# Input projection of a hybrid mLSTM / GLA / S5 layer: seven block products for two token blocks, intermediates in DRAM, recurrences in a second phase

## The chip, the cores and the metric

The kernel runs on one core of a Trainium2 chip. The metric is the device time of one execution in microseconds (us). TensorE (PE) multiplies; VectorE (DVE), ScalarE (ACT) and GpSimd (POOL) work elementwise; SyncE (SP) issues nearly all of the kernel's DMAs, in its program order. Each engine runs its own instructions in order and waits on semaphores.

## The reference

One layer on 2048 tokens of width 1024, all in fp32. Normalised tokens are projected to 10264 columns; three recurrences use parts of them; their gated outputs go through three branch matrices and an output matrix.

```python
proj = rmsnorm(x, norm_w) @ w_in                      # [2048,1024] @ [1024,10264]
(aq, ak, av, ao, ai, af, az, bq, bk, bv, ba, bz, cu, cz, g) = split(proj)
qk = silu(causal_dwconv([aq, ak], mlstm_conv))        # 4 taps, 1536 columns
ha = head_norm(mlstm_chunkwise(aq, ak, av, i_pre, logf))   # 4 heads of 192
ya = sigmoid(ao) * ha * silu(az)
yb = head_norm(gla_chunkwise(bq, bk, bv, log_a)) * silu(bz)  # 4 heads, 96 x 192
yc = gelu(s5_ssm(cu, ...)); yc = yc * sigmoid(yc @ s5_w_glu) * silu(cz)
merged = ga * (ya @ w_a) + gb * (yb @ w_b) + gc * (yc @ w_c)   # ga, gb, gc = sigmoid(g)
out = rmsnorm(x + merged @ w_out, final_norm)
```

## The kernel before

Tokens come in four blocks of 512. To keep fp32 accuracy in the fast matmul format, every operand is split into a high part (a rounding copy, on ScalarE) and a low part (the difference, on VectorE or GpSimd, `split`, line 84), and a product of two tiles takes three matmuls: high x high, high x low, low x high. `dense_fm` (line 110, matmuls in lines 122 to 124) gives a result with channels on partitions and 512 tokens in a row; `dense_tm` (line 128, lines 138 to 140) gives one with tokens on partitions, for the values and gates of the recurrences. Both go through the 1024 rows of `w_in` in eight k-tiles; `wload` (line 90) loads each k-tile of weights on SP and splits it, anew for each block.

First comes a stretch that makes the S5 preparation: the four blocks are normalised (`norm`, line 170), the S5 columns u and cz are projected (`proj_c`, with weights kept, names `keep`), the normalised and split blocks go to DRAM (`hnd`), and between them `s5_setup` and `s5_mats` (line 864; tiles P and W, on GpSimd in lines 888 to 891) build the S5 matrices. Then the blocks follow one another: for each, two `gla_pair`s and two `mlstm_pair`s (two heads each, chunks of 64 or 128 tokens), whose queries, keys, values and gates are projected right there, so that matmuls of a projection lie between the steps of a chunk; then three branches with their gates g, and the output projection (`tail`). A chunk of `mlstm_pair` (lines 586 to 646) makes scores (`sp`, line 590), weights them, multiplies by the values (`ni`, line 599) and the state (line 603), transposes the keys, and updates the state `cst` on VectorE (line 625). `s5_main` is mixed into the first block's branches.

The order on each engine is made by the Tile framework when the program is built: it takes the instructions in an order of its own from the code's and the buffers', and a tile's buffers (`bufs`) set how early a producer may run. Names in the rows are tiles: `d` is a PSUM result of a projection, `raw` loaded weights, `whi` and `wlo` their parts, `hn` normalised tokens, `yl` a branch's operand.

## Time and profile before

| | |
|---|---|
| Runs | 3009.79 and 3007.92 us, median 3008.86 |
| Profiled execution: span | 3011.8 us, 41837 instructions |
| TensorE busy | 2868.0 us (95%) |
| VectorE, ScalarE, GpSimd busy | 59%, 42%, 35% |
| DMA | 379.77 MB, mean 126 GB/s |

The page cuts the span into 40 slices of 75.3 us and gives each engine's busy share of a slice in tenths:

```profile
PE   7888899999889899999999999999999999999998
PEld 7667789887667789988888798988888798898886
DVE  7887767645465575665434467565434558556335
ACT  4323544433224554444333544444334554444334
POOL 6788543312240344331122145321122245221022
```

How to read it: where TensorE shows a 9, it is hardly ever waiting, whatever the others do; the slices with 7 and 8 lie at the start. Matmuls are pipelined, so the durations of neighbours overlap: the cost of one in a row of matmuls is the distance from one start to the next, not its duration. A mean over a group that mixes shapes says little, so groups are read by shape.

### The profile page before, as it was taken

The numbers are of one execution on the slowest core, as the hardware profiler recorded it, in microseconds if no ns is written. First come the engines' busy times: TensorE is split into PE (matmuls) and PEld (weight loads), VectorE is DVE, ScalarE is ACT, GpSimd is POOL, SyncE is SP. The second block draws the span as 40 slices with busy tenths as digits, with TensorE's granted clock in tenths as the row PEclk, the third lists the DMA queues.
The fourth block names the chain that finished last, engine by engine and source line by source line (L and its number), as shares of the span: only waits on it lengthen the run. The fifth ranks groups of instructions, "written<-read, shape, count | busy, mean of one in ns | idle before, by whom it ended". The sixth has DMA issues, their size and how long they took to land. (4 is left out here: it accounts for less than half of the span.)

```text
span 3011.8 us, 41837 instructions
## 1 busy us (share of the span) xinstructions
PE 2868.0 (95%) x14360; PEld 2452.7 (81%) x14360; DVE 1785.6 (59%) x3552; ACT 1257.2 (42%) x2512; POOL 1039.8 (35%) x1231
## 2 busy tenths in 40 slices
PE   7888899999889899999999999999999999999998
PEld 7667789887667789988888798988888798898886
DVE  7887767645465575665434467565434558556335
ACT  4323544433224554444333544444334554444334
POOL 6788543312240344331122145321122245221022
PEclk9999999999999999999999999999999999999999
DMA  8734323344777332334445332334445332334433
GB/s 262 254 116 153 108 65 90 91 115 132 210 217 231 121 114 74 86 89 117 135 119 161 120 91 74 94 89 118 138 119 174 98 104 66 99 88 141 148 116 103
DMA packets 279286, 379.77 MB, mean 126 GB/s; under 512 B 82656, under 2 KB 186000, under 8 KB 275744
## 3 DMA queue, kind: packets, MB, share of 16 engines
q1 hardware_dynamic: 273952, 368.70, 41.2%
q10 hardware_dynamic: 5120, 8.39, 1.1%
q8 instruction: 113, 1.85, 0.2%
q14 instruction: 101, 0.83, 0.1%
HBM read 302.33 MB, written 65.04 MB: 122 GB/s over the span
## 5 line engine op out<-in xcount | busy, mean ns | idle before, releaser
L86 DVE TENSOR_TENSOR wlo<-raw,whi 128x512 fp32r<-128x512 f32 (+2 forms) x736 | 548.2, 749 | 764.5 <-ACT whi L85 638.2
L85 ACT CAST whi<-raw 128x512 fp32r<-128x512 f32 (+2 forms) x736 | 421.2, 576 | 716.3 <-PE d L123 412.3
L122 PE MATMUL d<-hn,whi 128*128 128x512 f32 x1472 | 588.4, 400 | 10.1 <-ACT whi L85 8.1
L123 PE MATMUL d<-hn,whi 128*128 128x512 f32 x1472 | 581.7, 395 | 0.0
L124 PE MATMUL d<-hn,wlo 128*128 128x512 f32 x1472 | 553.1, 398 | 9.2 <-DVE wlo L86 8.8
L139 PE MATMUL d<-wlo,hn 128*128 128x384 f32 (+1 forms) x1280 | 442.2, 345 | 11.6 <-POOL wlo L105 6.3
L140 PE MATMUL d<-whi,hn 128*128 128x384 f32 (+1 forms) x1280 | 434.8, 340 | 0.0
L105 POOL TENSOR_TENSOR wlo<-raw,whi 128x384 fp32r<-128x384 f32 x208 | 234.0, 1125 | 518.0 <-ACT whi L104 358.3
L138 PE MATMUL d<-whi,hn 128*128 128x384 f32 (+1 forms) x1280 | 386.6, 348 | 6.9 <-DVE g L299 5.6
L122 PEld LDWEIGHTS d<-hn,whi 128*128 128x128 f32 x1472 | 278.9, 189 | 74.3 <-ACT whi L85 10.4
L124 PEld LDWEIGHTS d<-hn,wlo 128*128 128x128 f32 x1472 | 277.5, 189 | 73.1 <-DVE wlo L86 12.8
L123 PEld LDWEIGHTS d<-hn,whi 128*128 128x128 f32 x1472 | 278.6, 189 | 57.7 <-issue 1.3
L139 PEld LDWEIGHTS d<-wlo,hn 128*128 128x128 f32 x1280 | 243.1, 190 | 18.6 <-DVE wlo L86 7.8
L138 PEld LDWEIGHTS d<-whi,hn 128*128 128x128 f32 x1280 | 236.7, 190 | 15.8 <-DVE g L299 5.9
L140 PEld LDWEIGHTS d<-whi,hn 128*128 128x128 f32 x1280 | 243.2, 190 | 0.4
L669 POOL TENSOR_TENSOR yl<-yraw,yl 128x512 fp32r<-128x512 f32 x64 | 84.7, 1324 | 446.5 <-ACT yl L668 354.5
L122 PE MATMUL d<-yl,whi 128*128 128x512 f32 x512 | 205.6, 403 | 5.1 <-DVE sg L674 1.9
L123 PE MATMUL d<-yl,whi 128*128 128x512 f32 x512 | 202.8, 396 | 0.0
L124 PE MATMUL d<-yl,wlo 128*128 128x512 f32 x512 | 189.6, 399 | 4.7 <-DVE wlo L86 4.7
L104 ACT CAST whi<-raw 128x384 fp32r<-128x384 f32 x208 | 106.1, 510 | 198.4 <-PE d L140 138.5
L679 POOL TENSOR_TENSOR sg<-sg 128x512 f32<-128x512 f32 x64 | 92.8, 1479 | 107.3 <-DVE sg L674 107.3
L539 DVE SCALAR_TENSOR_TENSOR cacc<-craw,convw,cacc 128x512 f32<-128x512 f32 x144 | 120.9, 840 | 2.7
(311 smaller groups left out, 4846.7 us busy)
## 6 DMA issues: line engine op xcount, KB each, us to landing
raw<-in_w_in_dram SPq DMA_DIRECT2D x480, 192.0 KB
raw<-in_w_in_dram SPq DMA_DIRECT2D x232, 256.0 KB
yraw<-y_a SPq DMA_DIRECT2D x64, 256.0 KB
raw<-in_w_out_dram SPq DMA_DIRECT2D x64, 256.0 KB
hnd<-hn SPq DMA_DIRECT2D x6, 2048.0 KB
y_a<-ys SPq DMA_DIRECT2D x64, 192.0 KB
raw<-in_w_bb_dram SPq DMA_DIRECT2D x48, 256.0 KB
raw<-in_w_ba_dram SPq DMA_DIRECT2D x48, 256.0 KB
```

Source lines behind the costliest of these rows:

```text
L85: nc.scalar.copy(out=hi, in_=src)
L86: nc.vector.tensor_tensor(out=lo, in0=src, in1=hi.bitcast(F32), op=ALU.subtract)
L104: nc.scalar.copy(out=hi[:, 0:n], in_=raw[:, 0:n])
L105: nc.gpsimd.tensor_tensor(out=lo[:, 0:n], in0=raw[:, 0:n], in1=hi[:, 0:n].bitcast(F32), op=ALU.subtract)
L122: nc.tensor.matmul(pm, lhsT=hi[:, o:o + mm], rhs=rh[:, ts], start=(k == 0), stop=False)
L123: nc.tensor.matmul(pm, lhsT=hi[:, o:o + mm], rhs=rl[:, ts], start=False, stop=False)
L124: nc.tensor.matmul(pm, lhsT=lo[:, o:o + mm], rhs=rh[:, ts], start=False, stop=(k == nk - 1))
L138: nc.tensor.matmul(ps[c][:, 0:n], lhsT=lh[:, cs], rhs=hi[:, 0:n], start=(k == 0), stop=False)
L139: nc.tensor.matmul(ps[c][:, 0:n], lhsT=lh[:, cs], rhs=lo[:, 0:n], start=False, stop=False)
L140: nc.tensor.matmul(ps[c][:, 0:n], lhsT=ll[:, cs], rhs=hi[:, 0:n], start=False, stop=(k == nk - 1))
L539: nc.vector.scalar_tensor_tensor(out=acc, in0=raw[:, i:TB + i], scalar=convw[:, t, i:i + 1], in1=acc, op0=ALU.mult, op1=ALU.add)
L679: nc.gpsimd.tensor_tensor(out=acc[i], in0=acc[i], in1=sg[m], op=ALU.add)
```

## The change

The projection is done for two token blocks at once. Write the 1024 rows of `w_in` as two halves (k-tiles 0 to 3 and 4 to 7), and take two column tiles of 128: four weight blocks. The tokens of the two blocks, in the same two halves of the model's width, are four operand blocks. The four result blocks (two column tiles by two token blocks) would take eight block products; a known scheme (Strassen, in Winograd's form) takes seven, on sums and differences of the blocks. The sums of the operands are made once for a pair of blocks (`prep`): seven tiles `T[0..6]`, each with high and low part. The sums of the weights are made for every `quad` (lines 246 to 248 and 261), and the products are combined where PSUM is read (`p1`, `u2`, `u3`, `done`). There are 40 quads for a pair of blocks and one smaller tile for the gate columns (`gates`).

All projections now come in a first phase (`project`), whose results go to DRAM: gates g already through the tanh, convolved queries and keys, transposed values. The S5 matrices are made beside the quads of the first pair, `s5_main` beside those of the second. A second phase (`recur`) loads the results and runs recurrences, branches and tails; there the recurrences of block b + 1 are written ahead of the branches of block b.

```diff
+QUADS = ([("u", i) for i in range(2)] + [("cz", i) for i in range(2)] + [("bqk", i) for i in range(3)]
+         + [("bv", i) for i in range(3)] + [("bz", i) for i in range(3)] + [("aqk", i) for i in range(6)]
+         + [("av", i) for i in range(3)] + [("oz", i) for i in range(6)] + [("g", i) for i in range(12)])
...
+        T = [pool.tile([128, 4, 2, TB], F32R, name=f"T{i}") for i in range(7)]
...
+        def big(name):
+            return pool.tile([128, 4, TB], F32, tag="raw", name=name, bufs=2)
...
+        def prep(F, view, flat):
+
+            Q = big("G")
+            G.tensor_tensor(out=Q[:, 0], in0=F[:, 1], in1=F[:, 0], op=SB)
+            V.tensor_tensor(out=Q[:, 2], in0=F[:, 3], in1=F[:, 1], op=SB)
+            G.tensor_tensor(out=Q[:, 1], in0=F[:, 3], in1=Q[:, 0], op=SB)
+            V.tensor_tensor(out=Q[:, 3], in0=F[:, 2], in1=Q[:, 1], op=SB)
+            for i, s in enumerate((F[:, 0], Q[:, 1], F[:, 2], Q[:, 2], Q[:, 0], Q[:, 3], F[:, 3])):
+                hi, lo = view(T[i], 0), view(T[i], 1)
+                s = flat(s)
+                ACT.copy(out=hi, in_=s)
+                (G if i in (1, 3, 5) else V).tensor_tensor(out=lo, in0=s, in1=hi.bitcast(F32), op=SB)
+
+        def first_pair():
+            for c in range(NC):
+                F = big("F")
+                for m in range(2):
+                    def dst(g, pt, nw):
+                        V.tensor_tensor(out=F[:, 2 * g + m].rearrange("p (k t) -> p k t", k=4), in0=pt, in1=nw, op=M)
+                    norm(m, c, dst)
+                prep(F, lambda t, h: t[:, :, h, c * CH:(c + 1) * CH], lambda s: s.rearrange("p (k t) -> p k t", k=4))
+
+        def ahead(b, c):
+            def dst(g, pt, nw):
+                t = o("hs")[:, 0:TB].rearrange("p (k t) -> p k t", k=4)
+                V.tensor_tensor(out=t, in0=pt, in1=nw, op=M)
+                nc.sync.dma_start(out=hnd[b - 2, :, 4 * g:4 * g + 4, c * CH:(c + 1) * CH], in_=t)
+            norm(b, c, dst)
+
+        def second_pair():
+            for k in range(4):
+                F = big("F")
+                for m in range(2):
+                    for g in range(2):
+                        nc.sync.dma_start(out=F[:, 2 * g + m], in_=hnd[m, :, 4 * g + k])
+                prep(F, lambda t, h: t[:, k, h, :], lambda s: s)
+
+        def split(src, sub):
+            t = hl()
+            ACT.copy(out=t[:, 0], in_=src)
+            sub.tensor_tensor(out=t[:, 1], in0=src, in1=t[:, 0].bitcast(F32), op=SB)
+            return t
+
+        def product(ps, w, i, first, last):
+            for k in range(4):
+                hi, lo = w[:, 0, k, :], w[:, 1, k, :]
+                th, tl = T[i][:, k, 0, :], T[i][:, k, 1, :]
+                nc.tensor.matmul(ps, lhsT=hi, rhs=th, start=first and k == 0, stop=False, skip_group_check=True)
+                nc.tensor.matmul(ps, lhsT=hi, rhs=tl, start=False, stop=False, skip_group_check=True)
+                nc.tensor.matmul(ps, lhsT=lo, rhs=th, start=False, stop=last and k == 3, skip_group_check=True)
+
+        def quad(q, done):
+            raw = big("raw").rearrange("p a t -> p (a t)").rearrange("p (k c) -> p k c", k=8)
+            w = a["w_in"].rearrange("(k p) c -> p k c", p=128)
+            c1, c2 = columns(*q)
+            if c2 == c1 + 128:
+                nc.sync.dma_start(out=raw, in_=w[:, :, c1:c1 + 256])
+            else:
+                for j, c0 in enumerate((c1, c2)):
+                    nc.sync.dma_start(out=raw[:, :, 128 * j:128 * j + 128], in_=w[:, :, c0:c0 + 128])
+            a11, a12 = raw[:, 0:4, 0:128], raw[:, 4:8, 0:128]
+            a21, a22 = raw[:, 0:4, 128:256], raw[:, 4:8, 128:256]
+            s1 = pool.tile([128, 4, 128], F32, tag="s1", name="s1", bufs=1)
+            s2 = pool.tile([128, 4, 128], F32, tag="s2", name="s2", bufs=1)
+            G.tensor_tensor(out=s1, in0=a21, in1=a22, op=A_)
+            G.tensor_tensor(out=s2, in0=s1, in1=a11, op=SB)
+            G.tensor_tensor(out=a21, in0=a11, in1=a21, op=SB)
+            ps = [psa.tile([128, TB], F32, tag="pabc"[i + 1], name="p" + "abc"[i]) for i in range(3)]
+            pa, pb, pc = ps
+
+            def t2(name, bufs):
+                return pool.tile([128, TB], F32, tag=name, name=name, bufs=bufs)
+
+            product(pa, split(a11, V), 0, True, False)
+            p1 = t2("p1", 1)
+            ACT.copy(out=p1, in_=pa)
+            product(pb, split(s2, G), 1, True, False)
+            u2 = t2("u", 2)
+            V.tensor_tensor(out=u2, in0=pb, in1=p1, op=A_)
+            G.tensor_tensor(out=s2, in0=a12, in1=s2, op=SB)
+            product(pa, split(a12, V), 2, False, True)
+            done(0, 0, pa, None)
+            product(pb, split(a21, V), 3, False, False)
+            u3 = t2("u", 2)
+            V.tensor_tensor(out=u3, in0=pb, in1=p1, op=A_)
+            product(pc, split(s1, G), 4, True, False)
+            done(1, 1, pc, u3)
+            product(pb, split(a22, V), 5, False, True)
+            done(1, 0, pb, p1)
+            product(pc, split(s2, V), 6, False, True)
+            done(0, 1, pc, u2)
...
+            def g(n, m, ps, add):
+                t = o("sg")[:, 0:TB]
+                if add is not None:
+                    place(t, ps, add)
+                ACT.activation(out=t, in_=ps if add is None else t, func=AF.Tanh, scale=0.5)
+                nc.sync.dma_start(out=D["g_d"][2 * pr + m, 2 * i + n], in_=t)
...
+            def v(n, m, ps, add):
+                t = o("v")[:, 0:TB]
+                place(t, ps, add)
+                pt = psm.tile([128, NC, 128], F32, tag="m", name="ptv")
+                for c in range(NC):
+                    nc.tensor.transpose(pt[:, c, :], t[:, c * CH:(c + 1) * CH], ident)
+                s = o("vt")[:, 0:TB].rearrange("p (c d) -> p c d", c=NC)
+                ACT.copy(out=s, in_=pt)
+                e = 2 * i + n
+                nc.sync.dma_start(out=D["v_d"][0 if kind == "bv" else 1, 2 * pr + m, :, :, e * 128:(e + 1) * 128].rearrange("c t d -> t c d"), in_=s)
...
+        first_pair()
...
+        for j, y in enumerate(order):
+            if y is None:
+                gates(0)
+                continue
+            quad(y, enders(*y, 0))
+            if j >= 3 and j % 4 == 0 and j // 4 <= 8:
+                s5_mats(nc, a, s5, s5t, psm, ident, D["mat_d"], D["cs_d"], j // 4 - 1)
+            if j >= 22 and j % 2 == 0 and j < 38:
+                i = (j - 22) // 2
+                ahead(2 + i // 4, i % 4)
+        s5_cm.__exit__(None, None, None)
+        second_pair()
...
+        for j, y in enumerate(order):
+            if y is None:
+                gates(1)
+                continue
+            quad(y, enders(*y, 1))
+            if j >= 5 and j % 2 and (j - 5) // 2 < n5:
+                i = (j - 5) // 2
+                for st in (2, 1, 0):
+                    if 0 <= i - LAG[st] < nq:
+                        next(s5q[i - LAG[st]])
...
+    def rec(b):
+        gla_pair(b, 0)
+        gla_pair(b, 1)
+        mlstm_pair(b, 0)
+        mlstm_pair(b, 1)
+
+    rec(0)
+    for b in range(NB):
+        if b + 1 < NB:
+            rec(b + 1)
+        c_final(nc, a, mx, tl, b, dskip, u_d, y_d, z_d, y_a, dense_fm, split, full)
+        acc = {}
+        for bi in (2, 1, 0):
+            yl = {}
+            for f in range(2):
+                branch(b, acc, bi, f, yl)
+        tail(b, acc)
...
-    def start(b):
-        if b:
-            for g in range(2):
-                t = hn_p.tile([128, 4, 2, TB], F32R, tag="hn", name="hn", bufs=2)
-                for i in range(0, 4, HS):
-                    k = 4 * g + i
-                    nc.sync.dma_start(out=t[:, i:i + HS].bitcast(F32), in_=hnd[b, :, k:k + HS])
-                hn[g] = t
-        return gla_in(b)
...
-    gi = start(0)
-    n5 = nq + LAG[2]
-    for b in range(NB):
-        pool_lo[0] = True
-        gla_pair(b, 0, gi)
-        gla_pair(b, 1, gi)
-        tg = mlstm_gates(b)
-        mlstm_pair(b, 0, tg)
-        mlstm_pair(b, 1, tg)
-        pool_lo[0] = False
-        acc = {}
-        for i, bi in enumerate((1, 0, 2)):
-            sg = [gate(bi, f) for f in range(2)]
-            if i == (0 if b else 2):
-                c_final(nc, a, mx, tl, b, dskip, u_d, y_d, z_d, y_a, dense_fm, split, full)
-            if b == 0 and i == 2:
-                gi = start(1)
-            yl = {}
-            for f in range(2):
-                branch(b, acc, bi, f, sg[f], yl)
-                if b == 0 and i < 2:
-                    s5_steps(*(min(n5, -(-n5 // 4) * (2 * i + f + j)) for j in range(2)))
-        if b and b + 1 < NB:
-            gi = start(b + 1)
-        tail(b, acc)
```

`place` copies a PSUM result (ScalarE) or adds to it what `add` holds (VectorE), and `enders(kind, i, pr)` gives the function that finishes a quad of its kind and stores it. `ahead` normalises a chunk of the second pair and stores it in `hnd`.

Where it moves instructions, the order on an engine tells more. GpSimd, while the S5 matrices are made: before, its queue holds S5 work alone (lines 888 to 891; `P` and `W` are the matrices, `ma` and `mb` their products).

```order
L888 TENSOR_TENSOR ma_1534<-raw_1529,s5c_513 128x128
L889 TENSOR_TENSOR mb_1535<-raw_1529,s5c_518 128x128
L890 TENSOR_TENSOR W_1533<-ma_1534,mb_1535 128x4x16
L891 TENSOR_TENSOR W_1533<-ma_1534,mb_1535 128x4x16
L888 TENSOR_TENSOR ma_1534<-P_1532,s5c_502 128x128
L889 TENSOR_TENSOR mb_1535<-P_1532,s5c_504 128x128
```

In the changed kernel the same S5 work (lines 1006 to 1009) shares the queue with the quads' weight sums `s` and low parts `hl`.

```order
L222 TENSOR_TENSOR hl<-s_2243,hl 128x512
L1006 TENSOR_TENSOR ma_3654<-W_3653,s5c_460 128x128
L1007 TENSOR_TENSOR mb_3655<-W_3653,s5c_462 128x128
L246 TENSOR_TENSOR s_2413<-raw 128x512
L1008 TENSOR_TENSOR W_3653<-ma_3654,mb_3655 128x4x16
L1009 TENSOR_TENSOR W_3653<-ma_3654,mb_3655 128x4x16
L248 TENSOR_TENSOR raw<-raw 128x4x128
L1006 TENSOR_TENSOR ma_3654<-P_3652,s5c_460 128x128
L1007 TENSOR_TENSOR mb_3655<-P_3652,s5c_462 128x128
L1008 TENSOR_TENSOR P_3652<-ma_3654,mb_3655 128x4x16
L1009 TENSOR_TENSOR P_3652<-ma_3654,mb_3655 128x4x16
L1006 TENSOR_TENSOR ma_3654<-W_3653,s5c_460 128x128
```

So a quad's weight sums stand behind S5 steps, and the S5 steps behind the quad's.

SP where a new set of tokens is loaded: before, the next block's tokens (`hn`, line 734) come between loads of weights for work that is still running.

```order
L734 DMA hn<-hnd 128x2048 x2
L94 DMA raw<-in_w_glu_dram 128x512
L1001 DMA ut<-u_d 128x8x64
L1000 DMA yt<-y_d 128x8x64
L94 DMA raw<-in_w_in_dram 128x408 x2
L1001 DMA ut<-u_d 128x8x64
L94 DMA raw<-in_w_in_dram 128x408
L734 DMA hn<-hnd 128x2048 x2
L94 DMA raw<-in_w_in_dram 128x408 x4
```

In the changed kernel the second pair's tokens (`F`, line 216) come behind and among the last stores of the first pair's results, ahead of the next quads' weights.

```order
L326 DMA oz_d<-tz 128x512
L304 DMA z_d<-zt 128x512 x3
L216 DMA F<-hnd 128x512 x3
L304 DMA z_d<-zt 128x512
L216 DMA F<-hnd 128x512
L333 DMA g_d<-sg 128x512 x4
L304 DMA z_d<-zt 128x512 x2
L216 DMA F<-hnd 128x512 x4
L304 DMA z_d<-zt 128x512 x2
L216 DMA F<-hnd 128x512 x8
L238 DMA raw<-in_w_in_dram 128x8x256 x2
```

What moved: the loads of tokens stand behind stores that wait for the last quads' results.

TensorE in the mLSTM chunks: before, the steps of a chunk (`ni`, `sp`) have projection matmuls (lines 122 to 124) on both sides.

```order
L124 MATMUL d<-hn,wlo 128x512
L122 MATMUL d<-hn,whi 128x512
L599 MATMUL ni<-v,wt 128x193 x2
L603 MATMUL sp<-cst,ma 128x193
L603 MATMUL sp<-cst,mc 128x193
L603 MATMUL sp<-cst,mb 128x193 x2
L123 MATMUL d<-hn,whi 128x512
L124 MATMUL d<-hn,wlo 128x512
L122 MATMUL d<-hn,whi 128x512
```

In the changed kernel the chunks of the first block of the second phase follow each other with none between them (`pkm` transposed keys, `sa` and `sb` state updates, `pty` transposed outputs).

```order
L758 MATMUL sp<-cst,mq 128x193 x2
L766 MATMUL pkm<-ident,mk 128x128 x3
L772 MATMUL sa<-mv,mkt 128x193
L773 MATMUL sa<-mv,mkt 128x193
L775 MATMUL sb<-mv,mkt 64x193
L776 MATMUL sb<-mv,mkt 64x193
L601 MATMUL pty<-ident,y 128x128
L746 MATMUL sp<-mq,mk 128x128 x4
L601 MATMUL pty<-ident,y 128x128 x2
L758 MATMUL sp<-cst,mq 128x193 x4
L754 MATMUL ni<-mv,wt 128x193 x2
```

What moved: the projections that stood between the steps of these chunks are in the first phase now.

## Rows read from the trace of the kernel before

**Rows 1.** The page: busy time, share and count of each engine; bytes moved.

```profile
PE 2868.0 (95%) x14360; PEld 2452.7 (81%) x14360; DVE 1785.6 (59%) x3552; ACT 1257.2 (42%) x2512; POOL 1039.8 (35%) x1231
...
DMA packets 279286, 379.77 MB, mean 126 GB/s; under 512 B 82656, under 2 KB 186000, under 8 KB 275744
```

**Rows 2.** Stretches: length, then busy PE, PEld, DVE, ACT, POOL, clock, DMA, GB/s.

```profile
75.00:300.00 225.00, 194.68 (x887) 157.25 (x886) 180.87 (x527) 65.27 (x123) 187.15 (x424) 0.94 0.54 175
1050.00:2900.00 1850.00, 1824.13 (x9296) 1578.95 (x9295) 1040.41 (x1943) 806.72 (x1642) 538.21 (x470) 0.99 0.38 111
```

**Rows 3.** Lines, TensorE: form and count, busy and mean ns, idle before and releaser.

```profile
L122 PE MATMUL d<-hn,whi 128*128 128x512 f32 x1472 | 588.4, 400 | 10.1 <-ACT whi L85 8.1 <-DVE sg L674 0.9 <-ACT v L321 0.7
L139 PE MATMUL d<-wlo,hn 128*128 128x384 f32 x1152 | 396.7, 344 | 7.0 <-POOL wlo L105 6.3 <-DVE wlo L86 0.6
L139 PE MATMUL d<-wlo,hn 128*128 128x408 f32 x128 | 45.5, 356 | 4.6 <-DVE wlo L86 4.6
L122 PE MATMUL d<-hn,keep 128*128 128x512 f32 x96 | 39.6, 416 | 1.6 <-DVE zt L215 1.5
L123 PE MATMUL d<-hn,keep 128*128 128x256 f32 x64 | 19.7, 310 | 2.9 <-DVE hn L86 2.9
```

**Rows 4.** Timeline of TensorE in three places: start, duration, instruction and count.

```profile
66.69 0.39 PE L122 MATMUL d<-hn,whi 128*128 128x512 f32 x1
...
68.96 0.39 PE L122 MATMUL d<-hn,whi 128*128 128x512 f32 x1
...
1109.86 0.85 PE L138 MATMUL d<-whi,hn 128*128 128x384 f32 x4
1110.55 0.55 PE L409 MATMUL P<-gE 96*128 96x64 f32 x4
...
579.90 0.49 PE L304 MATMUL pty<-ident,y 128*128 128x128 f32 x3
```

**Rows 5.** Lines of the elementwise engines, and the first transposes in the timeline.

```profile
L85 ACT CAST whi<-raw 128x512 fp32r<-128x512 f32 x432 | 265.2, 619 | 498.3 <-PE d L123 349.4 <-PE d L140 52.3 <-issue 40.7
...
L184 ACT ACTIVATE xn<-xt 128x1024 f32<-128x1024 f32 x16 | 17.0, 1062 | 15.7 <-DMA xt<-in_x_dram 10.7 <-DVE xn L187 5.0
...
L669 POOL TENSOR_TENSOR yl<-yraw,yl 128x512 fp32r<-128x512 f32 x64 | 84.7, 1324 | 446.5 <-ACT yl L668 354.5 <-PE d L123 82.6 <-PE d L124 5.9
...
L86 DVE TENSOR_TENSOR wlo<-raw,whi 128x512 fp32r<-128x512 f32 x432 | 344.0, 800 | 469.6 <-ACT whi L85 360.7 <-PE d L123 71.5 <-PE d L124 33.4
...
L674 DVE SCALAR_TENSOR_TENSOR sg<-sg,d 128x512 f32<-128x512 f32 x96 | 59.7, 680 | 7.1 <-PE d L124 7.1
...
L539 DVE SCALAR_TENSOR_TENSOR cacc<-craw,convw,cacc 128x512 f32<-128x512 f32 x144 | 120.9, 840 | 2.7
...
8.34 1.97 PE L192 MATMUL pt<-ident,xn 128*128 128x128 f32 x8 [8.34 <-DVE xn L187]
```

**Rows 6.** First 340 us: tiles P and W by engine; two lines of VectorE.

```profile
0.00:340.00 340.00, 8.38 (x64) 5.54 (x64) 2.87 (x16) 4.96 (x8) 116.34 (x256) 0.95 0.59 192
...
0.00:340.00 340.00, 13.06 (x96) 9.24 (x96) 104.19 (x240) 0.95 0.59 192
...
L913 DVE TENSOR_TENSOR tm<-CS,en 128x8 f32<-128x8 f32 (+3 forms) x64 | 31.9, 498 | 0.0
...
L906 DVE TENSOR_TENSOR e<-CS 128x8 f32<-128x8 f32 x64 | 16.1, 252 | 1.5
```

**Rows 7.** Timeline of GpSimd and VectorE near 1012 us: start, duration, [wait <-releaser].

```profile
1011.74 1.29 POOL L669 TENSOR_TENSOR yl<-yraw,yl 128x512 fp32r<-128x512 f32 x1 [0.70 <-ACT yl L668]
...
1012.21 1.36 DVE L86 TENSOR_TENSOR wlo<-raw,whi 128x512 fp32r<-128x512 f32 x1 [0.76 <-ACT whi L85]
```

**Rows 8.** Timeline of one mLSTM chunk: its first matmul and its last state update.

```profile
580.22 0.39 PE L590 MATMUL sp<-ma 128*128 128x128 f32 x2
...
593.94 0.41 DVE L625 SCALAR_TENSOR_TENSOR cst<-cst,wp,sa 128x193 f32<-128x193 f32 x1
```

943 lines of the change are left out of this document (470 added, 473 removed).

## The prediction

> **What bounds the kernel now.** I read the page's first part first: TensorE is busy 2868.0 of 3011.8 us, VectorE 1785.6, ScalarE 1257.2, GpSimd 1039.8 [rows 1]. The reader is to see that one engine has 144 us of idle time and the others well over 1000. That is a share over stages, so the table of stretches comes next [rows 2]: from 1050 to 2900 us TensorE is busy 1824.13 of 1850 us (idle 1.4%) with VectorE at 56% and GpSimd at 29%; from 75 to 300 us, where the S5 matrices are made, it is busy 194.68 of 225 us (idle 13.5%) with VectorE at 80% and GpSimd at 83%. So in most of the kernel the number of matmuls sets the time, and where the two elementwise engines are both near 80% they begin to. These two stretches are my ends for everything below that the trace does not show.
>
> **The matmuls.** The input projection is lines 122 to 124 and 138 to 140, each line with the same count; [rows 3] has one of each form. Their durations overlap, so the price is the step from start to start: ten steps take 68.96 - 66.69 = 2.27 us, 0.227 each, for 512 columns; four take 1110.55 - 1109.86 = 0.69, 0.173 each, for 384 [rows 4]. Removed: 3 x (1472 + 96) = 4704 at 0.227 = 1067.8; 3 x 64 = 192 of half the length at half the step = 21.9; 3 x 1152 = 3456 at 0.173 = 597.9; 3 x 128 = 384 with 408 columns, 0.184 by length, 70.7. Together 1758 us. Added: a quad (two column tiles by two token blocks) issues 7 products x 4 k-tiles x 3 = 84 matmuls of 512 columns; 80 quads are 6720, the two gate tiles 96: 6816 x 0.227 = 1547 us. Transposes: 192 for the values in, 16 out, 176 x 0.11 us (three in 0.49 us with one length of 0.27: [rows 4]) = 19 us. Net 1758 - 1547 - 19 = **192 us less**, on the engine that sets the time. The branch and output matmuls stay. Busy time becomes 2868 - 192 = 2676 us.
>
> **The idle time, stage by stage.** It was 144 us; the new program's is built anew.
>
> Start. Every product needs all 512 columns of its operand, so all eight 128-token chunks must be normalised and combined before the first matmul. F and its combinations G turn in the same two buffers, so the four slices go one after the other. A slice costs ScalarE four passes of 1.06 us and seven casts of 0.6, some 8.5 us, and GpSimd five operations of 1.3 us, 6.6 us [rows 5]. The first transposes came at 8.34 us [rows 5]; 8 + 4 x 9 = 44, and the first quad's weights wait for F's buffer (1 MB, split, some 6 us more): about 50 us, of which 7 are transposes. Idle 45; 30 if slices overlap, 60 if not at all.
>
> Between the pairs. The operands of the second pair overwrite the first's and pass through the same two buffers, and the loads of F on SP are among the last stores. One of four slices can be made under the last quad; three remain, each a 1 MB load (6 us at the 175 GB/s of the second stretch in [rows 2]) and GpSimd's 6.6 us in series: 38 us, less what overlaps, plus weights. Nothing else is ready on TensorE. Idle 35; ends 20 (loads hidden: GpSimd's 3 x 6.6) and 55.
>
> Between the phases. The first GLA pair stands alone in TensorE's order until its levels are made. Idle 20; ends 10 and 40.
>
> First pair of blocks. TensorE needs 3408 x 0.227 = 774 us for its 40 quads and gates, some 800 with transposes and S5. VectorE, at the rows' means [rows 5]: 204 splits x 0.80 = 163, 200 additions out of PSUM x 0.68 = 136, 68 gatings x 0.68 = 46, 72 convolution steps x 0.84 = 60, S5 tables about 165 (four rows of at most 31.9, four of at most 16.1 [rows 6]), small ones 45: 615 us, 77%. GpSimd: six operations a quad, 240 x 1.32 = 317, and 116.34 + 104.19 = 221 for S5 [rows 6]: 538 us, 67%. These lie between the two stretches of [rows 2], nearer to the bad one; but most of the idle time there waited for transposed tokens, which here come far ahead. I take 6%, 50 us; ends 1.4% (11) and 13.5% (108).
>
> How GpSimd hurts VectorE is in the rows: a 512-column split takes 1.36 us where it starts 0.47 us into a GpSimd operation [rows 7], against 0.68 for an operation that reads PSUM [rows 5]. The Trainium skill (SBUF — State Buffer, "Who interferes with whom") says that a VectorE instruction with two SBUF inputs and a GpSimd instruction that reads SBUF exclude each other for the whole instruction. The rows agree: the split ends 0.54 us after GpSimd does. It speaks against this change, which adds 480 GpSimd operations beside the splits.
>
> Second pair. The same quads without the S5 preparation, VectorE near 60%: idle 2%, 15 us; ends 10 and 60.
>
> Second phase. The recurrences lose their cover. In the new order ten of the 32 mLSTM chunks have fewer than 13 dense matmuls since the chunk before (in the old one every chunk had at least 72), and about ten GLA chunks have under five. One chunk took from 580.22 to 594.35, 14.1 us, from its first matmul to its last state update [rows 8], loaded with other work; its own 20 TensorE instructions in the order, at 0.25 us, are 5. So an uncovered chunk loses up to 9 us; two pairs' steps and an idler VectorE shorten it, and I take 5, and 2 for GLA: 10 x 5 + 10 x 2 = 70 us. Ends 0 and 180. The last of it, 300 dense matmuls at the end, runs as before.
>
> Queues: SP issues 1362 transfers where it issued 1518. The new stores and loads of intermediates are some 145 MB, the weights and normalised tokens about 100 MB less; 380 becomes some 425 MB, at 146 GB/s where 126 is the mean now [rows 1]: hidden. Casts, PSUM copies and gatings on ScalarE (some 50% in the first phase) cost nothing while its queue is shorter than a product's 12 x 0.227 = 2.7 us; if not, the accumulation of the third product waits.
>
> **The sum.** 2676 + 45 + 35 + 20 + 50 + 15 + 70 = 2911 us, against the profiled 3011.8. The runs' median is 3008.9, 3 us below that execution, so I forecast **2908 us**, 3.4% less.
>
> **Rivals.**
> *The stalls don't come.* The old program, with every stage as mixed, idles 144 us; if the new order hides the uncovered chunks under the other pair and loses 1.4% in the quads, idle is 45 + 25 + 10 + 11 + 10 + 40 = 141: 2817, less 3 is **2814 us**. For it: the 1.4% in [rows 2]. Against: three new stretches with no dense work at all.
>
> *The shared access of VectorE and GpSimd bounds the first pair.* VectorE's splits, convolutions, S5 tables and SBUF gatings are 163 + 60 + 165 + 46 = 434 us, GpSimd's work 538; if none of it overlaps, 972 us against the 850 taken, and about 20 us in the second pair: 2908 + 122 + 20 = **3050 us**, slower than now. For it: [rows 7]. Against: the short S5 operations (rows of 0.5 us) stood beside VectorE at 80% without filling the 225 us. The rule of the Trainium skill's page named above would give this time if every operation held the access from end to end.
>
> *The recurrences set the second phase.* Their place is TensorE's queue: dense matmuls stand behind a chunk's wait. The mean cover is 1536 branch matmuls over 32 chunks, 48 x 0.227 = 10.9 us, with the chunk's own 5 us 16 us. At a chain of 14.1 us it fits with 2 us to spare; every us above 16 counts 32 times. VectorE, at 56% in the long stretch of [rows 2], would be near 75% here; if that makes the chain 22 us, 32 x 6 = 192 us: **3100 us**, slower by 3%. For it: thin margins and an order fixed beforehand. Against: without convolutions in the queue a chunk's VectorE steps come sooner.
>
> That the change doesn't remove the matmuls is no rival: the new order holds 6816 of them.
>
> **Chances.** Forecast with its neighbours, 2850 to 2965 us: 0.52. No stalls: 0.18. Shared access: 0.15. Recurrences: 0.15. About 2% is what a measurement of this kernel can tell from no change: 2949 and 3069 us. Of the forecast's 0.52 some 0.42 lies below 2949, and 0.18 joins it: faster 0.60. Slower is most of the last case and the tail of the third: 0.16. The rest, 0.24, is within 2%. Cases of both signs hold much of the chance, so the range is wide: 2770 to 3070 us, leaving out 0.04 below and 0.15 above; the likeliest case alone has 2850 to 2965.
>
> **What would show it.** TensorE's busy time near 2680 and its count lower by some 1700 rows' worth of dense matmuls; three holes in the slices, at the start, near 900 and near 1800 us; GpSimd's share up from 35% to over 50%; splits with means above 0.9 us in the first 900 us and near 0.75 in the next 850; in the second phase idle time before the matmuls of state and scores, released by VectorE. A first pair above 950 us would make the shared access right; a second phase above 1150 us the recurrences; holes under 20 us each and a quad at 19.1 us (84 x 0.227) throughout, the first rival.

## The result and the profile after

The changed kernel takes 3378.6 us (3378.0 and 3379.2) against 3008.9: ratio 1.123, 95% interval 1.120 to 1.126. The forecast was 2908 us, in a range of 2770 to 3070. The kernel is slower, and outside the range.

The page of the changed kernel, first part and three of the slices' rows (84.4 us a slice), beside [rows 1]:

```profile
PE 2906.8 (86%) x12617; PEld 2318.3 (69%) x12617; DVE 2200.4 (65%) x3757; ACT 1263.5 (37%) x2286; POOL 1677.1 (50%) x1592
...
PE   2678899999995689999899996988979897998888
...
POOL 6458736777345254444444444633544454455324
PEclk9789999999997889999999996776989688978879
```

TensorE issues 1743 matmuls and transposes fewer, as foreseen, but is busy longer, 2906.8 us where 2676 had been forecast. One part of that is the clock: from slice 25 on the granted clock is often 0.6 to 0.8, and further below the same eight matmuls count 2.05 us in one place and 3.80 in another. How the 231 us divide is not settled. The same execution in six stretches, as in [rows 2] (length, busy PE, PEld, DVE, ACT, POOL, granted clock, DMA share, GB/s): start, first pair's quads, switch of pairs, second pair's quads, switch of phases, second phase.

```profile
0.00:73.40 73.40, 16.16 (x66) 12.61 (x66) 57.58 (x155) 36.15 (x57) 42.43 (x50) 1.00 0.27 85
73.40:1053.90 980.50, 863.83 (x3684) 680.19 (x3684) 719.51 (x1350) 378.19 (x626) 593.02 (x767) 0.95 0.35 111
1053.90:1092.70 38.80, 0.41 (x3) 0.06 (x1) 24.64 (x22) 13.88 (x23) 23.57 (x16) 0.54 0.38 127
1092.70:2027.50 934.80, 866.88 (x3715) 698.79 (x3716) 593.23 (x766) 364.01 (x603) 410.40 (x281) 0.96 0.39 119
2027.50:2041.20 13.70, 0.40 (x2) 0.00 (x0) 2.34 (x7) 0.63 (x1) 2.37 (x2) 0.59 0.75 205
2041.20:3375.90 1334.70, 1159.07 (x5152) 926.64 (x5152) 803.07 (x1460) 470.66 (x976) 605.32 (x479) 0.81 0.46 146
```

Against the terms of the prediction. The second pair's is 774 of products, some 26 of other work as in the first and 15 idle; the second phase's is what the sum of 2911 leaves. The last two columns are the part in which TensorE is idle (length less busy time).

| | forecast | measured | over | idle, forecast | idle, measured |
|---|---|---|---|---|---|
| start | 52 | 73.4 | 21 | 45 | 57 |
| first pair | 850 | 980.5 | 131 | 50 | 117 |
| switch of pairs | 35 | 38.8 | 4 | 35 | 38 |
| second pair | 815 | 934.8 | 120 | 15 | 68 |
| switch of phases | 20 | 13.7 | -6 | 20 | 13 |
| second phase | 1139 | 1334.7 | 196 | 70 | 176 |

The idle time is 469 us instead of 235. So of the 465 us too many one half is idle time and the other half busy time.

The two switches, which looked most like holes, were sized well; the stretches of work were not. Two more views of them. The waits of TensorE in the second phase (who <- whom: us in total, times, longest):

```profile
PE pty L601 <- ACT y L798: 52.3, 15, 5.4
PE pty L601 <- ACT y L709: 25.2, 10, 6.4
PE P L635 <- DVE gE L665: 21.3, 12, 3.3
```

The longest are not for scores or state, which the prediction had expected, but for transposes of a chunk's normalised output (`pty`): a result that no later chunk needs, standing ahead of the next chunk in TensorE's queue. And what stands in the first 107 us of the second pair:

```profile
PE pa L229 <- ACT hl L221: 45.0, 2, 38.4
PE ptg L458 <- ACT gat L455: 21.0, 2, 18.3
```

The 38.4 is the switch. The transposes `ptg` of the mLSTM gates belong to the gate tile: around it no quad's product starts for 51.1 us in the first pair (at 131 us) and 48.8 us in the second (at 1139 us). The prediction counted the two gate tiles as 96 matmuls and no more. ScalarE in the second hole loads function tables between the steps of the gates' chain, and a quad's cast (`hl`) stands in the middle of it:

```profile
1143.31 1.28 ACT L438 ACT_TABLE_LOAD   x1
1144.60 0.63 ACT L438 ACTIVATE ls<-ls 4x512 f32<-4x512 f32 x1
1145.25 1.28 ACT L418 ACT_TABLE_LOAD   x1
...
1151.02 0.61 ACT L221 CAST hl<-s 128x512 fp32r<-128x512 f32 x1
```

### The profile page after: what moved, and what is told of

It reads as the page before. It is cut to its first block, busy times and chain, and to the rows that moved or that the text cites. A ratio compares the mean times of both kernels' runs of the same rounds, so it can differ in the third digit from the quotient of the medians.

```text
span 3375.9 us, 38126 instructions
## 1 busy us (share of the span) xinstructions
PE 2906.8 (86%) x12617; PEld 2318.3 (69%) x12617; DVE 2200.4 (65%) x3757; ACT 1263.5 (37%) x2286; POOL 1677.1 (50%) x1592
## 5 line engine op out<-in xcount | busy, mean ns | idle before, releaser
L222 POOL TENSOR_TENSOR hl<-s,hl 128x512 fp32r<-128x512 f32 x160 | 221.6, 1385 | 411.9 <-ACT hl L221 406.8
L229 PE MATMUL pb<-T,hl 128*128 128x512 f32 x960 | 386.5, 403 | 40.5 <-DVE u L260 18.6
L231 PE MATMUL pb<-T,hl 128*128 128x512 f32 x960 | 383.5, 400 | 1.6 <-POOL hl L222 1.1
L230 PE MATMUL pb<-T,hl 128*128 128x512 f32 x960 | 381.7, 398 | 0.0
L222 DVE TENSOR_TENSOR hl<-raw,hl 128x512 fp32r<-128x512 f32 x320 | 290.6, 909 | 136.6 <-ACT hl L221 124.9
L229 PE MATMUL pa<-T,hl 128*128 128x512 f32 x640 | 266.1, 416 | 91.3 <-ACT hl L221 72.7
L231 PE MATMUL pa<-T,hl 128*128 128x512 f32 x640 | 262.1, 410 | 22.7 <-DVE hl L222 22.5
L221 ACT CAST hl<-raw 128x512 fp32r<-128x512 f32 x320 | 196.5, 617 | 212.3 <-PE pa L231 71.1
L221 ACT CAST hl<-s 128x512 fp32r<-128x512 f32 x244 | 150.7, 618 | 299.7 <-PE pb L231 197.0
L231 PE MATMUL pc<-T,hl 128*128 128x512 f32 x640 | 253.7, 396 | 9.2 <-POOL hl L222 9.2
L230 PE MATMUL pa<-T,hl 128*128 128x512 f32 x640 | 259.2, 405 | 0.0
L229 PE MATMUL pc<-T,hl 128*128 128x512 f32 x640 | 254.2, 397 | 0.0
L230 PE MATMUL pc<-T,hl 128*128 128x512 f32 x640 | 252.1, 394 | 0.0
L229 PEld LDWEIGHTS pb<-T,hl 128*128 128x128 f32 x960 | 183.6, 191 | 94.8 <-DVE u L260 23.8
L553 POOL TENSOR_TENSOR wlo<-raw,whi 128x512 fp32r<-128x512 f32 x104 | 142.5, 1371 | 170.0 <-ACT whi L551 102.9
L551 ACT CAST whi<-raw 128x512 fp32r<-128x512 f32 x208 | 128.0, 619 | 232.5 <-PE d L574 108.8
L231 PEld LDWEIGHTS pb<-T,hl 128*128 128x128 f32 x960 | 183.3, 191 | 45.0 <-POOL hl L222 4.9
L230 PEld LDWEIGHTS pb<-T,hl 128*128 128x128 f32 x960 | 183.4, 191 | 38.6
```

The lines of the kernel that those rows point to most:

```text
L221: ACT.copy(out=t[:, 0], in_=src)
L222: sub.tensor_tensor(out=t[:, 1], in0=src, in1=t[:, 0].bitcast(F32), op=SB)
L229: nc.tensor.matmul(ps, lhsT=hi, rhs=th, start=first and k == 0, stop=False, skip_group_check=True)
L230: nc.tensor.matmul(ps, lhsT=hi, rhs=tl, start=False, stop=False, skip_group_check=True)
L231: nc.tensor.matmul(ps, lhsT=lo, rhs=th, start=False, stop=last and k == 3, skip_group_check=True)
L551: ACT.copy(out=hi, in_=src)
```

## The experiments

Each experiment is one execution of the changed kernel with an edit. Stretches begin and end where the changed kernel's do: first product, 40 quads, switch, 40 quads, first matmul of the recurrences. The kernel before, run beside them on the same chips, took 3006 to 3020 us, so differences of ten us between runs on different chips say little.

**Eight products in the new arrangement.** What do the seven products bring by themselves?

```diff
-T = [... for i in range(7)]          # sums s1, s2, p1, u2, u3 go too
+T = [... for i in range(4)]
+hs = [split(w_, e) for w_, e in ((a11, V), (a12, V), (a21, V), (a22, G))]
+for i, (n, m) in enumerate(((0, 0), (0, 1), (1, 0), (1, 1))):
+    for h in range(2):
+        product(ps, hs[2 * n + h], 2 * h + m, h == 0, h == 1)
+    done(n, m, ps, None)
```

(Split weights have 8 buffers instead of 5.)

> The same kernel with eight block products instead of seven: four operand tiles instead of seven, no sums of weights or operands, four splits a quad instead of seven, and each result one chain of eight k-tiles. 96 matmuls a quad instead of 84. Phases, order and stores stay, S5 preparation included. Theory 1 (TensorE sets the quads; the seven products bring their eighth): 80 x 12 x 0.227 = 218 us more in the two pairs, less what the start (4 operand splits instead of 7 and no sums: 15 us), the switch of pairs (20 us) and the waits in the first quads (50 us) give back: total 3480 to 3560. Theory 2 (the elementwise work that seven products need sets the quads): the two pairs take no longer than now, 1955 us, total 3250 to 3390.

3370.8 us. Its first five stretches:

```profile
0.00:45.90 45.90, 15.40 (x66) 11.96 (x66) 32.75 (x115) 30.59 (x49) 19.66 (x38) 0.90 0.48 154
45.90:1019.40 973.50, 936.14 (x4164) 762.76 (x4164) 424.70 (x1100) 321.75 (x518) 275.54 (x559) 0.97 0.36 113
1019.40:1034.20 14.80, 0.44 (x3) 0.05 (x1) 4.87 (x8) 6.25 (x11) 4.11 (x4) 0.62 0.82 259
1034.20:2021.20 987.00, 954.99 (x4187) 782.08 (x4188) 307.79 (x486) 304.27 (x493) 106.98 (x80) 0.98 0.37 113
2021.20:2035.60 14.40, 2.15 (x10) 1.52 (x8) 1.65 (x6) 1.18 (x2) 2.38 (x2) 0.68 0.72 189
```

960 matmuls more, 960 x 0.227 = 218 us, and the second phase starts at 2035.6 instead of 2041.2 us. Theory 2 holds: what seven products save on TensorE goes into their elementwise work. Start and switch take 28 and 24 us less with eight, the first pair's quads 7 less, and only the second pair's 52 more. It also separates the two halves of the change: without the seven-product scheme, the new arrangement alone is some 358 us slower (3370.8 against 3013.2 beside it).

**The quads' sums and splits on VectorE.** Is it the amount of elementwise work, or the engine it stands on?

```diff
-            G.tensor_tensor(out=s1, in0=a21, in1=a22, op=A_)
+            V.tensor_tensor(out=s1, in0=a21, in1=a22, op=A_)   # and the other three sums
-            product(pb, split(s2, G), 1, True, False)
+            product(pb, split(s2, V), 1, True, False)          # and split(s1, G)
```

> In the quads, the four sums of weights and the two splits that stand on GpSimd go to VectorE (240 operations a pair); the S5 preparation and everything else stay. Theory 1 (shared access: a split takes 0.69 us alone and 1.02 to 1.18 us beside a GpSimd operation, so VectorE gets back much of what it takes on): second pair 935 us to 890 to 930, first pair no longer than now, total 3320 to 3380. Theory 2 (the amount of work on VectorE sets the first pair's quads: 74% busy before, with 6 x 0.69 = 4 us more a quad over 90%): first pair 40 to 120 us longer, second within 20 us, total 3400 to 3510.

3268.9 us, 110 less. The two pairs, and two lines of VectorE in the first pair, with this edit (first fence) and without it (second):

```profile
71.00:973.10 902.10, 842.09 (x3683) 673.95 (x3684) 719.56 (x1592) 383.05 (x626) 275.65 (x520) 0.96 0.38 121
...
1012.10:1910.40 898.30, 854.11 (x3715) 695.97 (x3716) 618.58 (x1006) 366.63 (x603) 58.22 (x41) 0.97 0.41 124
...
L222 DVE TENSOR_TENSOR hl<-raw,hl 128x512 fp32r<-128x512 f32 x160 | 114.2, 714 | 17.4 <-ACT hl L221 17.0
L266 DVE TENSOR_TENSOR u<-pb,p 128x512 f32<-128x512 f32 x40 | 27.5, 686 | 23.4 <-PE pb L231 23.0
```

```profile
L222 DVE TENSOR_TENSOR hl<-raw,hl 128x512 fp32r<-128x512 f32 x160 | 142.5, 891 | 56.5 <-ACT hl L221 53.7 <-POOL s L261 1.2 <-POOL W L1009 0.7
L266 DVE TENSOR_TENSOR u<-pb,p 128x512 f32<-128x512 f32 x40 | 27.4, 686 | 52.5 <-PE pb L231 52.5
...
L222 POOL TENSOR_TENSOR hl<-s,hl 128x512 fp32r<-128x512 f32 x160 | 221.6, 1385 | 411.9 <-ACT hl L221 406.8 <-DMA y_d<-y 4.9
```

The second fence is the changed kernel (its last line over the whole run). In the first pair VectorE does 242 instructions more in the same busy time (719.56 for 719.51 us), because each is faster: the split takes 714 ns for 891. On GpSimd the same split took 1385. The first pair gets 78 us shorter, the second 37. Theory 1 holds, and its range of 3320 to 3380 was too timid; theory 2, which took VectorE's busy share for work, falls. The rule of the Trainium skill (SBUF — State Buffer, "Who interferes with whom"), by which a VectorE instruction with two SBUF inputs and a GpSimd instruction that reads SBUF exclude each other, agrees with these rows: the addition `u`, which reads one input from PSUM, takes 686 ns in both runs.

Two things are not separated. The edit ends the overlap on the shared access, and it also takes operations of 1385 ns out of a quad's own chain: without it ScalarE's casts waited 31.2 us in the first pair for one of the sums (`s`, line 247), with it 7.2. How the 110 us divide between the two is open. That TensorE itself waited for GpSimd's splits only 10 us in the first pair, and under 1 in the second, speaks for the shared access as the larger part.

And with the sums on VectorE the two pairs take 1800 us together, where eight products took 1960 (with one split of each quad still on GpSimd): there the seven products seem to bring most of their 218 us.

**S5 preparation tied to its quads.** One-column copies (`now` is the quad's `p1[:, 0:1]`) hold each S5 step back until its quad has begun; a fourth holds back the setup:

```diff
+    V.tensor_copy(out=P[:, 0, 0, 0, 0:1], in_=now)
+    G.tensor_copy(out=ma[:, 0, 0, 0:1], in_=now)
+    V.tensor_copy(out=CS[:, 0, 0, 0:1], in_=now)
```

> Ties the S5 preparation to the quads beside which it is written: three one-column copies from a quad's first result make the S5 setup start after the first quad and the eight matrix steps at quads 4, 8, ... 32, where now most of the S5 work on VectorE (108 of 128 table steps) is done in the first 450 us. Same work, same output. Theory 1 (VectorE, busy 405 of the first 450 us, is what the first quads wait for, since the S5 tables stand early in its queue): start 73 to about 62 us, first pair 981 to 860 to 910 us, total 3250 to 3310. Theory 2 (VectorE and GpSimd hurt each other through shared access to memory wherever the S5 work stands): the first pair stays at 950 to 1000 us, total 3350 to 3390.

3430.0 us, longer than either theory said. The start fell to 65.6 us, and VectorE is busy 343 instead of 405 of the first 450 us, but the first pair:

```profile
65.60:1087.90 1022.30, 880.01 (x3683) 694.51 (x3684) 764.58 (x1429) 380.85 (x628) 592.66 (x787) 0.93 0.34 107
```

42 us longer, with VectorE busy 45 us more; part of that is the S5 setup, which stood ahead of the first product and now stands behind it. Start and first pair together are 34 us longer, and the rest of the kernel 18. That S5 stands early was not the fault; in this run, where it is spread over more quads, it costs more. Theory 1 falls, and its rival had no such loss either.

**The gate tile, moved and tied.** First to the end of each pair:

```diff
-        order = [("u", 0), ("u", 1), None]
+        order = [("u", 0), ("u", 1)]
-        order += full + rest2
+        order += full + rest2 + [None]
```

> In each pair the gate tile is done after the quads instead of third; nothing else changes. Theory 1 (TensorE stands some 49 us without a product in each pair, near 131 and 1139 us, because transposes of the mLSTM gates wait in its queue for a chain on ScalarE with its table loads and on VectorE): the hole of the first pair falls into the switch of pairs, which costs 39 us anyway, and that of the second into the switch of phases; 45 to 80 us less in all, total 3300 to 3335. Theory 2 (the hole only moves and adds to those two switches): total 3365 to 3390.

3310.1 us: 68 less, inside theory 1's range. Second pair, switch of phases and second phase:

```profile
1080.30:1950.00 869.70, 840.28 (x3655) 683.42 (x3656) 546.06 (x690) 325.89 (x556) 391.99 (x274) 0.99 0.42 126
1950.00:2020.00 70.00, 21.27 (x62) 13.57 (x61) 43.17 (x83) 40.74 (x48) 13.86 (x8) 0.60 0.23 67
2020.00:3308.30 1288.30, 1127.51 (x5152) 905.31 (x5152) 784.15 (x1460) 469.63 (x976) 609.16 (x480) 0.84 0.48 151
```

The number comes out, the places do not. The second pair begins 12 us earlier; it goes from 935 to 870 us, but the switch of phases from 14 to 70. So the holes gave 12 and 9 us, and the other 47 lie in the second phase, 1288 us for 1335. Its first 1500 matmuls take 390 us in both runs; the gain comes behind them. TensorE's instructions stand in another order there; why that is shorter is not shown.

Then left third, with only its transposes tied to the next quad (`gat` gets a buffer of its own for it):

```diff
+            V.tensor_copy(out=pt[:, 0, 0:1], in_=now)          # ahead of the transposes of gat
```

> The gate tile stays third in each pair, but the transposes of the mLSTM gates are tied to the next quad's first result (a one-column copy from it ahead of them), so that in TensorE's order 24 to 36 products stand between the gates' matmuls and their transposes. Theory 1 (TensorE's queue stands behind these transposes): each hole goes from 49 us to 15 to 28, total 3300 to 3340. Theory 2 (the chain on ScalarE and VectorE keeps the quads' own splits and copies waiting, so the wait moves to the next product): total 3350 to 3390.

3372.2 us: theory 2. The holes are still 44 and 41 us. The waits for the gates' transposes are gone in the second pair, and others stand there. The largest, next to that of the switch:

```profile
PE pg L229 <- ACT hl L221: 10.3, 2, 6.7
```

So TensorE's queue is not the main cause: the gates' chain keeps ScalarE, which makes these casts (`hl`), and VectorE from the next weights.

**Output transposes one chunk later.**

```diff
             emit_y(b, 3 * p, c, y, gate)        # now only puts it on a list
+            flush(1)                            # writes all but the latest; the same in gla_pair
```

> In the second phase the output transposes of a chunk (and what follows them) are written one chunk later, behind the next chunk's own matmuls; nothing else changes. Theory 1 (the largest waits of TensorE there, 52 + 25 us, are those of the transposes for ScalarE's normalised output, with the next chunk's matmuls queued behind them, and the clock falls meanwhile): the waits go and the phase shrinks by 77 to 150 us, total 3225 to 3300. Theory 2 (the chain through the state is as long as the chunk, so the wait moves to the next matmul): total 3350 to 3390.

3261.1 us: 117 less, theory 1. The second phase, and the waits for the transposes, 21 us where they were 77:

```profile
2039.20:3259.30 1220.10, 1098.73 (x5152) 890.55 (x5152) 787.73 (x1460) 471.43 (x976) 606.36 (x479) 0.87 0.51 160
...
PE pty L610 <- ACT y L809: 15.4, 4, 4.0
PE pty L610 <- ACT y L718: 5.5, 3, 3.4
```

**Useless matmuls against the clock.** Consecutive mLSTM chunks in the timeline of the changed kernel (start, duration, instruction and count): the first line is of a chunk with dense matmuls around it, the others of two that have none:

```profile
2284.77 2.05 PE L758 MATMUL sp<-cst,mq 128*128 128x193 f32 x8
...
2299.22 1.65 PE L754 MATMUL ni<-mv,wt 128*128 128x193 f32 x4
...
2303.86 1.01 PE L773 MATMUL sa<-mv,mkt 128*128 128x193 f32 x2
2304.80 0.90 PE L776 MATMUL sb<-mv,mkt 128*64 128x193 f32 x2
2308.87 0.47 PE L601 MATMUL pty<-ident,y 128*128 128x128 f32 x1 [3.17 <-ACT y L798]
2309.14 1.79 PE L746 MATMUL sp<-mq,mk 128*128 128x128 f32 x8
2310.86 0.69 PE L601 MATMUL pty<-ident,y 128*128 128x128 f32 x2
2311.34 3.80 PE L758 MATMUL sp<-cst,mq 128*128 128x193 f32 x8
```

The same eight state matmuls take 2.05 us in the first and 3.80 in the last, where TensorE had waited 3.17 us for the output a little before. The granted clock was 0.84 from 2275 to 2300 us and 0.50, the lower level (1.2 GHz), from 2300 to 2325; over the phase it is 0.81. So useless matmuls, whose results nothing reads, were added to hold the clock up:

```diff
+    def idle(ps, n, cols):
+        for i in range(n):
+            nc.tensor.matmul(ps, lhsT=fill[:, 0:128], rhs=fill[:, 0:cols], start=True, stop=True, ...)
         pt = psm.tile([128, 3, 128], F32, tag="m", name="pty")
+        idle(pt, 16, 384)                       # 6 in the light fill
         P = psm.tile([128, 2 * NC, 64], F32, tag="m", name="P")
+        idle(P[:, 0:6, :], 8, 384)              # 4 in the light fill
```

> Adds useless matmuls of 384 columns to the recurrences of the second phase: 16 ahead of the output transposes of each of the 64 chunks, 8 ahead of each of the 56 GLA levels with a decay tile, 1472 in all; at the step of 0.173 us for 384 columns they are 255 us of TensorE work. The output is not touched. Theory 1 (the granted clock: in the uncovered chunks TensorE stands at 1.2 GHz, and the matmuls inside the chain take twice their time): the mean clock of the second phase goes from 0.81 to over 0.92, an uncovered mLSTM chunk from 16 us to 12 to 14, and the phase, 1348 us now, gets shorter although work is added: 1220 to 1320, total 3250 to 3350. Theory 2 (the chain over VectorE and ScalarE sets the phase, the clock falls in time that is lost anyway): the phase keeps its length or gets longer by up to the added work: 1348 to 1600, total 3380 to 3630.

> The changed kernel with 608 useless matmuls of 384 columns in the second phase, 6 ahead of the output transposes of each of 64 chunks and 4 ahead of each of 56 GLA levels: 105 us of TensorE work at full clock, two fifths of the first fill, which took the clock of the phase from 0.81 to 0.97 and left its length (1331 for 1335 us). Theory 1 (the clock costs real time; the first fill paid it back with too much work): the phase gets shorter, 1230 to 1310 us, total 3275 to 3355. Theory 2 (waits set the phase, the clock falls in their shadow): 1335 to 1440 us, total 3378 to 3480.

> Late output transposes and the 608 useless matmuls of the light fill together; each alone gave 3261 and 3278 us, phase 1220 and 1235 us. Theory 1 (the clock, 0.87 in the phase with late transposes, costs time of its own): phase 1130 to 1200 us, total 3170 to 3240. Theory 2 (what the fill gave was the end of the same waits): phase 1220 to 1320, total 3260 to 3360.

3374.2, 3278.0 and 3262.4 us. The second phases, in this order:

```profile
2041.20:3372.40 1331.20, 1275.79 (x6624) 1088.85 (x6624) 783.17 (x1460) 469.47 (x976) 592.54 (x479) 0.96 0.47 147
```

```profile
2036.30:3276.10 1239.80, 1165.12 (x5760) 963.39 (x5760) 794.29 (x1460) 468.53 (x976) 609.62 (x479) 0.93 0.50 157
```

```profile
2035.30:3260.60 1225.30, 1151.42 (x5760) 952.42 (x5760) 794.84 (x1460) 468.94 (x976) 606.80 (x479) 0.94 0.51 159
```

The clock went from 0.81 to 0.96 and 0.93, and 255 us of work cost nothing: the first fill kept the length, which is its theory 2 (3374 us, just under its range). The light fill won 100 us and so fell into the range of its theory 1. But on top of late transposes, where the clock also rose, from 0.87 to 0.94, it won nothing, and theory 2 of the third run holds. So what the light fill won was most likely the same as what late transposes win, the waits for them: the added matmuls stand in these waits, and in many mLSTM chunks the transposes came to stand behind the next chunk's scores.

What the clock is worth by itself the runs do not give. In the third run against late transposes alone, 105 us of fill raised TensorE's busy time by 53 us (1098.7 to 1151.4) and lowered its idle time by 47 (121 to 74). So by these numbers the other matmuls got some 52 us shorter, and the phase 5 us longer: whether the faster matmuls paid for the fill, or neither mattered because waits set the length, is open. That holding the clock up shortens the phase is not shown.

**Two streams; splits of the second phase on VectorE.** The two GLA pairs of a block beside its two mLSTM pairs, with late transposes:

```diff
     def rec(b):
-        gla_pair(b, 0) ... mlstm_pair(b, 1)
+        two = [chain.from_iterable((f(b, 0), f(b, 1))) for f in (gla_pair, mlstm_pair)]
+        ...                                     # three GLA steps, one mLSTM chunk, in turn
```

> Second phase only: the two GLA pairs of a block and its two mLSTM pairs, which don't depend on each other, are written as two streams side by side (three GLA steps, then one mLSTM chunk), so that the three shared PSUM banks turn in that order; output transposes one chunk late in each stream, as in the run before. Same work, same output. Theory 1 (one chain at a time leaves TensorE waiting at 1.2 GHz; the other stream is cover): the second phase, 1335 us as changed and 1220 with the late transposes alone, goes to 1030 to 1150, mean clock over 0.9, total 3070 to 3190. Theory 2 (the three PSUM banks or VectorE, busy 63% of the phase, hold both streams back): 1200 us or more, total 3240 or more.

3243.2 us, 18 less than late transposes alone, on another chip; the second phase is at the edge of theory 2:

```profile
2040.10:3241.30 1201.20, 1090.61 (x5152) 878.12 (x5152) 808.43 (x1460) 467.71 (x976) 605.27 (x478) 0.88 0.51 162
```

And by itself, on the changed kernel:

```diff
-        (V if par[0] % 2 else G).tensor_tensor(out=lo, in0=src, in1=hi.bitcast(F32), op=SB)
+        V.tensor_tensor(out=lo, in0=src, in1=hi.bitcast(F32), op=SB)     # and the branch operands' splits
```

> Second phase only: all splits of weights and branch operands on VectorE; now 104 weight splits and 64 operand splits stand on GpSimd at 1.37 us. Theory 1 (a GpSimd operation slows VectorE's, 0.69 to 1.1 us a split here too): second phase 1335 us to 1260 to 1310, total 3300 to 3355. Theory 2 (the phase is set by one recurrence chain and the clock; the splits are off that chain): 1325 to 1345, total 3365 to 3390. Theory 3 (VectorE, 63% busy, takes on 168 x 0.69 = 116 us and becomes the bound): total 3400 to 3450.

3319.9 us; the phase 1282 for 1335: theory 1.

```profile
2036.20:3318.00 1281.80, 1128.97 (x5152) 904.15 (x5152) 841.26 (x1636) 469.94 (x976) 376.88 (x303) 0.84 0.49 152
```

**Most of the branch matmuls left out.**

```diff
-        nk, k0, wb = ((6, 0, a["w_ba"]), (6, 6, a["w_bb"]), (4, 12, a["w_bc"]))[bi]
+        nk, k0, wb = ((1, 0, a["w_ba"]), (1, 6, a["w_bb"]), (1, 12, a["w_bc"]))[bi]
```

> The changed kernel with branches that multiply only the first of their six, six and four k-tiles (the output leaves out the others); recurrences, gates, output projection and the whole first phase as they are. It takes out 4 x 312 = 1248 matmuls of 512 columns, 283 us at 0.227, and 104 weight splits and 52 operand splits. Theory 1 (the recurrences' chains set the phase, the branches only fill it): second phase 1335 us to 1200 to 1335, total 3240 to 3380. Theory 2 (work on the engines sets it): 1335 less 283, 1000 to 1080 us, total 3040 to 3120.

3196.4 us, between the theories:

```profile
2041.20:3194.60 1153.40, 929.07 (x3904) 720.40 (x3904) 737.23 (x1408) 384.32 (x820) 468.73 (x375) 0.72 0.43 133
```

283 us of matmuls less, with their splits, shorten the phase by 181, to 1153 us. So the branches are not mere filling, and not the bound either. What is left has 1248 dense matmuls, as many as were taken out, and the recurrences' own. TensorE is idle 224 us of it, 49 more than in the changed kernel. The recurrences without any dense work were not run.

**All together.** VectorE for the sums and splits (second phase's too, and the operands' but for one split in seven), two streams, late transposes; the gate tile tied, or last; then four PSUM banks for the recurrences:

```diff
-    psd = pool_of("psd", bufs=5, space=PSUM)
+    psd = pool_of("psd", bufs=4, space=PSUM)
-    psm = pool_of("psm2", bufs=3, space=PSUM)
+    psm = pool_of("psm2", bufs=4, space=PSUM)
```

> Together: the quads' sums and splits on VectorE, operand sums too, second-phase splits on VectorE, tied gate transposes, two streams with late output transposes. If the gains add (110 + 50 + 135 and 0 to 50 of the phase-2 splits and 10 of the start): 3020 to 3085, level with the kernel before at best. If they overlap, above all if VectorE becomes the bound of the second phase: 3100 to 3200.

> As the version with two streams and everything on VectorE, with the gate tile last in each pair instead of tied. The tied transposes gave 6 us, the gate tile last 68 us. If that is worth the same here: total 3040 to 3080, still behind the kernel before (3006 to 3016). If the holes at the switches grow by what the quads gain: 3100 to 3130.

> The version with the gate tile last and all other changes, with four PSUM banks for the recurrences and four for the dense products, three and five now. Theory 1 (a chunk takes seven tiles in turn out of three banks, which ties the two streams to each other): second phase 1203 us to 1080 to 1170, total 2985 to 3075. Theory 2 (the chain through the state and VectorE sets it; a dense group of four has then no bank to start the next one in): 1195 to 1260, total 3100 to 3165.

3115.5, 3107.1 and 3097.4 us: the first two as in the worse case of their expectations, the third just below its theory 2. With one recurrence after the other instead of two streams the first was 3118.3, so the streams gave 3 us there, and the light fill made the second 3125.6. No version beats the kernel before; the last is some 3% slower. The last one's second phase:

```profile
1906.20:3095.60 1189.40, 1059.24 (x5152) 854.24 (x5152) 831.02 (x1636) 468.06 (x976) 373.08 (x302) 0.89 0.52 164
```

1189 us, where late transposes alone gave 1220: in this phase the gains overlap. What keeps it there is not settled. TensorE is idle 130 us of it and VectorE is busy 70%. With the fourth bank the phase was 12 us shorter, but on another chip, where the kernel before was 8 us faster too.

## Why the prediction was wrong

**The matmuls** were counted right: 12617 instructions for 14360, and a quad without waits took 19.2 us (84 x 0.227 = 19.1). Eight products in the same arrangement need 218 us more on TensorE and gain it back elsewhere, so the saving was there and was spent. TensorE's busy time was not right: 2676 us took the old busy time less 192 us at the steps of undisturbed rows, and 2907 were measured. The sum has no term for matmuls that take longer where they follow a wait or a fall of the clock.

**The idle terms of the quads**, 50 and 15 us, failed; 117 and 68 were measured, in pairs that are 131 and 120 us too long. This has two causes. The shared access was priced and put among the rivals at 0.15: 122 us in the first pair and 20 in the second. Taking GpSimd out of the quads, which also shortens their chain, gave 78 and 37. So the price, 142 against 115, was about right, with too much in the first pair and too little in the second, where the quads' own six GpSimd operations stand as well. The splits took 891 ns in the first pair, close to the mark of over 900, and 927 in the second, where 750 had been expected. The argument against the rival, that S5's short operations had not filled the stretch of [rows 2], did not bear on operations of 512 columns, and [rows 7] showed those.

The other cause was not in the prediction at all: **the gate tile**, a chain of scans, activations and table loads (1.28 us each in the timeline) on ScalarE and VectorE. In the kernel before it lay between other work; now it stands in the quads' queue. It makes two holes of some 50 us, some 8 of each the tile's own matmuls. What the holes cost is less clear: moving the tile gave 21 us in the first phase, and 47 in the second that are not explained.

**The term for the second phase** (70 idle, of which 5 us a chunk) failed: 176 us are idle, and the phase is 196 us too long. The rival that the recurrences set this phase had given 192, and its mark, a phase above 1150 us, is there. Its mechanism was half of it. The chains hold a part of the phase: 283 us of matmuls less shorten it by 181 only. But the largest wait was for the output transposes, 117 us in the run that moved them, and the releaser was ScalarE, not VectorE. The granted clock had no term either. It fell to 0.81 here, yet the runs do not show that holding it up shortens the phase.

**The rivals were taken as alternatives.** One sits in the first phase, the other in the second, and nothing keeps them from coming together. Forecast plus both is 2908 + 142 + 192 = 3242 us; taken one at a time they capped the range at 3100. Two gate holes of some 40 would bring the sum to 3322, 1.7% from the result, but that is partly luck: by places it has some 35 us too much in the first pair and 60 too little in the second, and moving the tile did not give 40 a hole.

**The start** was 21 us longer than its 52: transposes waited for VectorE there, on which S5's setup stands too, and the tied S5 brought 8 of it back. The two switches were right within 6 us.

## What to carry to other kernels

A saving on the bound engine is worth what the other engines leave of it: count the elementwise operations that the scheme adds, per product, at the price they have beside each other, and ask on which engine they stand. Work that was cover somewhere has a price where it is taken from; a phase of recurrences without dense work has to be costed as chains, with every result that stands in a queue ahead of the next step. And rivals with different places add up.
